# A 90-degree rotation on one core: pairs of slabs turned in place, and 24 transfers in place of 40

## The chip, the core and the metric

The kernel runs on one core of a Trainium2 chip. The core has a matrix engine (TensorE, not used here), VectorE (DVE in the profile), ScalarE (ACT), GpSimd (POOL) and SyncE (SP), and 16 transfer engines (DMA) that move data between the chip's main memory (HBM) and the core's own memory (SBUF, 128 partitions). A second small memory, PSUM, has 128 partitions of 16 KB; transfers here go between HBM and SBUF only, so what is in PSUM must be copied to SBUF before it is stored.

The metric is device time in microseconds, lower is better. Before the change it is 123.27 us, the median of 3 runs (123.24 to 123.33).

## The reference

```python
def setup_inputs():
    batch, c, h, w = 32, 3, 256, 256
    return {"x": np.random.randn(batch, c, h, w).astype(np.float32)}

def reference(x: np.ndarray) -> np.ndarray:
    return np.rot90(x, k=-1, axes=(-2, -1)).astype(np.float32)
```

Each of the 96 images of 256 x 256 single-precision numbers is turned by 90 degrees clockwise. Nothing is computed; 25.17 MB are read, rearranged and written back.

## The kernel before

**Slabs.** Eight images (2048 rows of 1 KB, 2.1 MB) are a slab; there are 12 (`n_slabs`). In SBUF a slab is 128 partitions of 16 KB. Which rows of an image stand in one partition is a choice. With short rows (`short`, 8 image rows) one contiguous piece in HBM is 8 KB and a partition takes two pieces, from two groups of four images (`i`). With long rows (`long`, 16 image rows) a piece is 16 KB and a partition takes one. A long transfer covers every second partition (`units[n][i::I]`), so a slab needs two of them, one for the even and one for the odd partitions.

**Turning.** VectorE's transpose instruction turns blocks of 32 partitions by 32 elements. Its access patterns pick, for each output column, the elements that belong together, and write them back in reversed order. If a slab is loaded in short rows, its turned form stands in long rows, and the other way round: a single slab has 8 KB pieces on one side, the load or the store. Only two slabs turned together as a pair can have 16 KB pieces on both. `turn(n)` (lines 102 to 118) does this with instructions of 128 x 2048 elements, 24 in all.

**Homes.** A turned slab is written where the slab before it was (`home = [turned0] + units[:last]`, line 100): slab 0 goes to PSUM, slab 1 to where slab 0 was, and so on. Slabs 0, 1 and 2 are loaded short and stored long, 3 to 7 loaded long and stored short. Slabs 8 and 9, and 10 and 11, are pairs (`both`, `paired`), loaded and stored long; a pair is turned in four instructions into the place of the pair before it. At the end ScalarE copies slab 0 out of PSUM (line 146) into the place of the last slab, in two halves, and it is stored last.

**Order.** All transfers are issued by SP, one after another, into one queue, which the 16 transfer engines serve in that order. The loads come first, 23 of them (the first half of the last slab is cut into 14 KB and 2 KB rows at line 94). A scheduling note at lines 139 and 140 keeps the first store behind the last loads. Then come the 17 stores: slabs 4, 3, 5, 6, 7 (short, line 132), 1 and 2 (long, line 130), the pairs (lines 124 and 127) and slab 0. A tile framework adds the waits: VectorE waits for the loads of the slab that it turns and, where a new slab overwrites what it has just read, for its own earlier instruction; a store waits for the transposes; and each transfer takes one of eight semaphores in turn, so it waits for the transfer eight before it.

Of the kernel before, what the change touches and what calls it, by code (L numbers as in the profile page):

```python
# [1 line left out]

# [4 lines left out]

@with_exitstack
def kernel(
    ctx: ExitStack,
    tc: tile.TileContext,
    x: bass.AP,
    out: bass.AP,
):

    nc = tc.nc
    fp32 = mybir.dt.float32

    B, C, H, W = x.shape
    P = nc.NUM_PARTITIONS
    RL, RS = 16, 8  # L50
    I = 2
    Q = P * RS // H
    n_slabs = B * C // (Q * I)
    last = n_slabs - 1
    F = RS * W
    long_st = (0, 1, 2)
    both = (8, 10)
    paired = [n + a for n in both for a in range(2)]

    rows_in = x.rearrange("b c h w -> (b c h) w")  # L60
    rows_out = out.rearrange("b c h w -> (b c h) w")

    def short(rows):
        return rows.rearrange("(n i p r) w -> n p i (r w)", i=I, p=P, r=RS)

    def long(rows):
        return rows.rearrange("(n i m r) w -> n i m (r w)", i=I, m=P // I, r=RL)

    ld_short, ld_long, st_short, st_long = short(rows_in), long(rows_in), short(rows_out), long(rows_out)

    units = [None] * n_slabs
    adjacent = [(3, 7), (8, 9), (10, 11)]
    pairs = []
    for us in adjacent + [(u,) for u in range(n_slabs) if all(u not in us for us in adjacent)]:
        pool = ctx.enter_context(tc.tile_pool(name=f"unit{us[0]}", bufs=1))
        held = pool.tile([P, len(us), I * F], fp32, name=f"u{us[0]}")
        for j, u in enumerate(us):
            units[u] = held[:, j]
        pairs.append(held)
    psum = ctx.enter_context(tc.tile_pool(name="psum", bufs=1, space=bass.MemoryType.PSUM))  # L80
    turned0 = psum.tile([P, I * F], fp32, name="turned0")

    def fours(t):
        return t.rearrange("p (i f) -> p i f", i=I)

    for n in (0, 1, 2, 3, 7, 4, 5, 6, *range(8, n_slabs)):
        if n in (1, 2):
            nc.sync.dma_start(out=fours(units[n]), in_=ld_short[n])
            continue
        for i in range(I):  # L90
            if n in long_st:
                ld = nc.sync.dma_start(out=fours(units[n])[:, i], in_=ld_short[n][:, i])  # L92
            else:
                cuts = (0, 14 * W, RL * W) if (n, i) == (last, 0) else (0, RL * W)
                for f0, f1 in zip(cuts, cuts[1:]):
                    ld = nc.sync.dma_start(out=units[n][i::I, f0:f1], in_=ld_long[n, i][:, f0:f1])
                    if f1 == 14 * W:
                        mark = ld

    home = [turned0] + units[:last]  # L100

    def turn(n):
        if n in long_st:
            src = fours(units[n]).rearrange("p i (r g c) -> p c r g i", r=RS, c=RL)
            dst = home[n].rearrange("p (c k r) -> p c r k", c=RL, r=RS)[:, :, ::-1, ::-1]
            parts, step = 2, RL // 2
        elif n in paired:
            if n not in both:
                return
            src = pairs[both.index(n) + 1].rearrange("p a (r g c) -> p c r g a", r=RL, c=RL)  # L110
            dst = pairs[both.index(n)].rearrange("p i (c k r) -> p c r k i", c=RL, r=RL)[:, :, ::-1, ::-1, :]
            parts, step = 4, RL // 4
        else:
            src = units[n].rearrange("p (r g c) -> p c r g", r=RL, c=RS)
            dst = fours(home[n]).rearrange("p i (c k r) -> p c r k i", c=RS, r=RL)[:, :, ::-1, ::-1, :]
            parts, step = 2, RS // 2
        for h in range(parts):
            nc.vector.transpose(out=dst[:, h * step : (h + 1) * step], in_=src[:, h * step : (h + 1) * step])  # L118

    def store(n):  # L120
        if n in paired:
            first = n if n in both else n - 1
            if n == first:
                nc.sync.dma_start(out=st_long[n].transpose([1, 0, 2]), in_=pairs[both.index(n)][::I])
                return
            for i in range(I):
                nc.sync.dma_start(out=st_long[n, i], in_=pairs[both.index(first)][n - first :: I, i])
        elif n in long_st:
            for i in range(I):
                nc.sync.dma_start(out=st_long[n, i], in_=home[n][i::I])  # L130
        else:
            return nc.sync.dma_start(out=st_short[n], in_=fours(home[n]))

    for n in range(both[0]):
        turn(n)
    for n in (4, 3, 5, 6, 7, 1, 2):
        st = store(n)
        if n == 4:
            tc.add_manual_dep(st.ins, mark.ins.name, mybir.DependencyInfo(
                mybir.DependencyClass.Sync, mybir.DependencyReason.SCHED_ONLY), reason="stores after loads")  # L140
    for n in range(both[0], n_slabs):
        turn(n)
        store(n)

    for i in range(I):
        nc.scalar.copy(out=fours(units[last])[:, i], in_=fours(turned0)[:, i])  # L146
    home[0] = units[last]
    store(0)


# [1 line left out]
_INS = ['x']  # L152
_OUTS = [((32, 3, 256, 256), 'float32')]


# [23 lines left out]
```

## Time and profile before

| what | value |
|---|---|
| device time, median of 3 runs | 123.27 us (123.24 to 123.33) |
| span of the profiled execution, first to last instruction | 121.4 us |
| around the span (123.27 less 121.43, if the profiled execution is a median one; the page gives no device time of its own) | 1.84 us |
| VectorE busy | 90.5 us, 24 instructions, from 8.25 to 99.1 us |
| ScalarE busy | 4.9 us, 3 instructions |
| transfer engines' share of the span | 98.0% |
| moved | 25.17 MB read, 25.17 MB written, 414 GB/s over the span |

The profile is one execution, recorded by the chip. Its page gives the busy time of each engine, then the span in 40 slices with the busy share of each engine in tenths, the share of the 16 transfer engines, and the GB/s that they moved. Then it follows the chain of work that ended last back from the end, from each instruction to what released it. "issue" in it is time in which an engine waited for nothing that the profile shows. Lines of groups of instructions read: line of the kernel, engine, operation, output<-input with their sizes, count | busy us, mean ns of one | idle time before them. A window's line reads: from:to, length, busy time and count for VectorE, ScalarE and GpSimd, clock, share of the transfer engines, GB/s. The trace behind the page also has the moments at which each transfer's 16 parts have landed, and the start, duration and size of each packet that a transfer engine moved.

### The profile page before, as it was taken

The page shows a single profiled execution, that of the slowest core. Times are in us where ns is not written, and L with a number is a line of the kernel's source. Part 1 is how long each engine was busy: PE and PEld are TensorE (multiplying, and loading weights), DVE is VectorE, ACT ScalarE, POOL GpSimd, SP SyncE. Part 2 cuts the span into 40 slices and gives each one's busy share as a digit, 9 for nine tenths or more (in the row PEclk, how much of TensorE's full clock was granted, in tenths as well). Part 3 has the DMA queues.
Part 4 walks back from the last instruction along what each step waited for, and adds up shares of the span by engine and source line. Part 5 has one row for each costly group of instructions (what it writes and reads, how often), then busy time and mean ns, then how long its engine had stood idle before and what let it go on. Part 6 is the DMA issues. An engine that isn't in the chain of part 4 may idle for free.

```text
span 121.4 us, 134 instructions
## 1 busy us (share of the span) xinstructions
DVE 90.5 (75%) x24; ACT 4.9 (4%) x3; POOL 0.2 (0%) x4
## 2 busy tenths in 40 slices
DVE  0029999999999999999999999999999960000000
ACT  0000000000000000000040000000000038000000
POOL 0000000000000000000000000000000000000000
DMA  3999999999999999999999999999999999999994
GB/s 84 416 432 424 426 459 432 432 432 426 426 432 426 416 421 432 421 426 450 403 424 426 426 429 429 421 432 424 464 426 432 432 432 432 432 432 432 432 432 178
DMA packets 4800, 50.33 MB, mean 414 GB/s; under 512 B 640, under 2 KB 640, under 8 KB 704
## 3 DMA queue, kind: packets, MB, share of 16 engines
q1 hardware_dynamic: 4800, 50.33, 98.0%
HBM read 25.17 MB, written 25.17 MB: 414 GB/s over the span
## 4 chain that ended last, share of the span: by engine, by line
DVE 55%; issue 17%; DMA 6%; DVEq 3%; ACT 2%; ACTq 1%; SPq 0%
DVE u L118 50%; DVE turned L118 6%; DMA u<-in_x_dram 6%; DVEq L174 3%; ACT u L146 2%; ACTq L174 1%; SPq L92 0%; DVEq L118 0%
## 5 line engine op out<-in xcount | busy, mean ns | idle before, releaser
L118 DVE STREAM_TRANSPOSE u<-u 128x2048 f32<-128x2048 f32 x22 | 83.4, 3861 | 0.3
L118 DVE STREAM_TRANSPOSE turned<-u 128x2048 f32<-128x2048 f32 x2 | 7.1, 3584 | 8.3 <-DMA u<-in_x_dram 8.3
L146 ACT COPY u<-turned 128x2048 f32<-128x2048 f32 x2 | 3.6, 1869 | 35.6 <-DVE u L118 35.6
L146 ACT ACT_TABLE_LOAD x1 | 1.3, 1283 | 62.3 <-DMA u<-in_x_dram 62.3
L163 POOL MEMSET const-uint8-127<- 128x1 uint8 x1 | 0.1, 103 | 0.0
L163 POOL MEMSET const-bfloat16-1.0<- 128x1 bf16 x1 | 0.1, 101 | 0.0
L163 POOL MEMSET const-float32-0.0<- 128x1 f32 x1 | 0.1, 99 | 0.2 <-issue 0.2
L163 POOL MEMSET const-float32-1.0<- 128x1 f32 x1 | 0.1, 99 | 0.0
## 6 DMA issues: line engine op xcount, KB each, us to landing
u<-in_x_dram SPq DMA_DIRECT2D x19, 1024.0 KB, 19.6
out_dram<-u SPq DMA_DIRECT2D x7, 2048.0 KB, 16.3
out_dram<-u SPq DMA_DIRECT2D x10, 1024.0 KB, 18.3
u<-in_x_dram SPq DMA_DIRECT2D x2, 2048.0 KB, 13.7
u<-in_x_dram SPq DMA_DIRECT2D x1, 896.0 KB, 19.3
u<-in_x_dram SPq DMA_DIRECT2D x1, 128.0 KB, 17.2
```

The lines of the kernel that those rows point to most:

```text
L118: nc.vector.transpose(out=dst[:, h * step : (h + 1) * step], in_=src[:, h * step : (h + 1) * step])
L146: nc.scalar.copy(out=fours(units[last])[:, i], in_=fours(turned0)[:, i])
L163: nc = _bacc.Bacc("TRN2", target_bir_lowering=False, num_devices=1)
L174: with _tile.TileContext(nc) as tc:
```

## The change

All 12 slabs are now six pairs, each one tile of 128 x 2 x 4096 elements. PSUM holds two tiles of 8 KB a partition, `spare[0]` and `spare[1]`.

- Slabs 1 and 0 are loaded in short rows, one transfer each, and turned one at a time: slab 1 into the two spares, slab 0 into the place of slab 1; ScalarE then copies the spares to where slab 0 was. Their stores are in 16 KB rows.
- The other ten slabs are loaded as five pairs in 16 KB rows, two transfers a pair, each for every second partition with two pieces (one of each slab, 2 MB apart in HBM). Each pair is turned in its own place, in quarters: the first quarter goes to a spare, the next three each move into the quarter just emptied, and ScalarE copies the spare into the last one in two instructions. The pairs use the two spares in turn.
- All stores are 2.1 MB each in 16 KB rows, in the order of the pairs, after all loads.

SP issues 12 loads and 12 stores, where it issued 23 and 17. VectorE still has 24 transposes, now in other shapes and with a wait for its own previous instruction within a pair. ScalarE has 12 copies in place of 2. The cut of the last slab, the scheduling note and the moving homes are gone.

```diff
-    RL, RS = 16, 8
+    R = 16
...
     def long(rows):
-        return rows.rearrange("(n i m r) w -> n i m (r w)", i=I, m=P // I, r=RL)
+        return rows.rearrange("(n a i m r) w -> n i m a (r w)", a=2, i=I, m=P // I, r=R)
...
-    adjacent = [(3, 7), (8, 9), (10, 11)]
...
-    turned0 = psum.tile([P, I * F], fp32, name="turned0")
+    pairs = [
+        ctx.enter_context(tc.tile_pool(name=f"pair{n}", bufs=1)).tile([P, 2, E], fp32, name=f"u{n}")
+        for n in range(n_slabs // 2)
+    ]
+    spare = [psum.tile([P, E // 2], fp32, name=f"spare{h}") for h in range(2)]
...
-    for n in (0, 1, 2, 3, 7, 4, 5, 6, *range(8, n_slabs)):
...
-                cuts = (0, 14 * W, RL * W) if (n, i) == (last, 0) else (0, RL * W)
...
+    for s, home in ((1, 0), (0, 1)):
+        nc.sync.dma_start(
+            out=pairs[0][:, home].rearrange("p (i f) -> p i f", i=I), in_=ld_short[s])
+    for n in range(1, len(pairs)):
         for i in range(I):
+            nc.sync.dma_start(out=pairs[n][i::I], in_=ld_long[n, i])
...
+    def turn_slab(src, dsts):
+        s = src.rearrange("p (i r g c) -> p c r g i", i=I, r=R // I, c=R)
+        for h, d in enumerate(dsts):
+            d = d.rearrange("p (c k r) -> p c r k", c=hw, r=R // I)[:, :, ::-1, ::-1]
+            nc.vector.transpose(out=d, in_=s[:, h * hw : (h + 1) * hw])
+
+    turn_slab(pairs[0][:, 0], spare)
+    turn_slab(pairs[0][:, 1], [pairs[0][:, 0, : E // 2], pairs[0][:, 0, E // 2 :]])
+    for h in range(2):
+        nc.scalar.copy(out=pairs[0][:, 1, h * E // 2 : (h + 1) * E // 2], in_=spare[h])
+
+    def turn_pair(n):
+        u = pairs[n]
+        src = u.rearrange("p a (r g c) -> p c r g a", r=R, c=R)
+        dst = u.rearrange("p i (c k r) -> p c r k i", c=R, r=R)[:, :, ::-1, ::-1, :]
+        held = spare[n % 2]
+        low, high = slice(0, hw), slice(hw, R)
+        nc.vector.transpose(
+            out=held.rearrange("p (i c k r) -> p c r k i", i=I, c=hw, r=hw)[:, :, ::-1, ::-1, :],
+            in_=src[:, low, low])
+        for c, r in ((low, high), (high, high), (high, low)):
+            nc.vector.transpose(out=dst[:, c, r], in_=src[:, c, r])
+        for i in range(I):
+            nc.scalar.copy(
+                out=u[:, i, : E // 2].rearrange("p (c r) -> p c r", r=R)[:, :, hw:],
+                in_=held[:, i * E // 4 : (i + 1) * E // 4].rearrange("p (c r) -> p c r", r=hw))
+
+    for n in range(1, len(pairs)):
+        turn_pair(n)
+    for n in range(len(pairs)):
+        for a in range(2):
+            if n == 0:
+                st = rows_out[: 2 * P * R].rearrange("(s i m r) w -> i m s (r w)", s=2, i=I, r=R)[a]
             else:
+                st = rows_out.rearrange("(n a i m r) w -> n a m i (r w)", a=2, i=I, m=P // I, r=R)[n, a]
+            nc.sync.dma_start(out=st, in_=pairs[n][a::2])
```

More of the change, by code (lines that the diff above doesn't have):

```diff
@@ L49 @@
     P = nc.NUM_PARTITIONS
-    RL, RS = 16, 8
+    R = 16
     I = 2
[L52 to L58, printed above, removed]
+    E = R * W
+    n_slabs = B * C * H // (P * R)
+    hw = R // 2
     rows_in = x.rearrange("b c h w -> (b c h) w")
@@ L63, in short @@
     def short(rows):
-        return rows.rearrange("(n i p r) w -> n p i (r w)", i=I, p=P, r=RS)
+        return rows.rearrange("(n i p r) w -> n p i (r w)", i=I, p=P, r=R // I)
     def long(rows):
-        return rows.rearrange("(n i m r) w -> n i m (r w)", i=I, m=P // I, r=RL)
-    ld_short, ld_long, st_short, st_long = short(rows_in), long(rows_in), short(rows_out), long(rows_out)
-    units = [None] * n_slabs
-    adjacent = [(3, 7), (8, 9), (10, 11)]
[L73 to L79, printed above, removed]
@@ L80 @@
-    psum = ctx.enter_context(tc.tile_pool(name="psum", bufs=1, space=bass.MemoryType.PSUM))
-    turned0 = psum.tile([P, I * F], fp32, name="turned0")
-    def fours(t):
-        return t.rearrange("p (i f) -> p i f", i=I)
-    for n in (0, 1, 2, 3, 7, 4, 5, 6, *range(8, n_slabs)):
-        if n in (1, 2):
-            nc.sync.dma_start(out=fours(units[n]), in_=ld_short[n])
-            continue
-        for i in range(I):
-            if n in long_st:
-                ld = nc.sync.dma_start(out=fours(units[n])[:, i], in_=ld_short[n][:, i])
-            else:
-                cuts = (0, 14 * W, RL * W) if (n, i) == (last, 0) else (0, RL * W)
[L95 to L147, printed above, removed]
@@ L148 @@
-    store(0)
+        return rows.rearrange("(n a i m r) w -> n i m a (r w)", a=2, i=I, m=P // I, r=R)
+    ld_short, ld_long, st_long = short(rows_in), long(rows_in), long(rows_out)
+    pairs = [
+        ctx.enter_context(tc.tile_pool(name=f"pair{n}", bufs=1)).tile([P, 2, E], fp32, name=f"u{n}")
+        for n in range(n_slabs // 2)
+    ]
+    psum = ctx.enter_context(tc.tile_pool(name="psum", bufs=1, space=bass.MemoryType.PSUM))
+    spare = [psum.tile([P, E // 2], fp32, name=f"spare{h}") for h in range(2)]
```

## The prediction

> **What bounds the kernel now.** I read the engine totals first, then the busy share by slices, then the chain that ended last, then windows cut at the landings of the transfers. First the totals and the slices (a slice is 3.03 us):
>
> ```profile
> DVE 90.5 (75%) x24; ACT 4.9 (4%) x3; POOL 0.2 (0%) x4
> ...
> DVE  0029999999999999999999999999999960000000
> ...
> DMA  3999999999999999999999999999999999999994
> GB/s 84 416 432 424 426 459 432 432 432 426 426 432 426 416 421 432 421 426 450 403 424 426 426 429 429 421 432 424 464 426 432 432 432 432 432 432 432 432 432 178
> DMA packets 4800, 50.33 MB, mean 414 GB/s; under 512 B 640, under 2 KB 640, under 8 KB 704
> q1 hardware_dynamic: 4800, 50.33, 98.0%
> ```
>
> The transfer engines are full from the first slice to the last; VectorE (DVE), the only busy compute engine, stops at 99.1 us, 22 us before the end. Every byte must cross: 25.17 MB in, 25.17 MB out. So the chain that ended last must not be read as "VectorE is the limit":
>
> ```profile
> DVE 55%; issue 17%; DMA 6%; DVEq 3%; ACT 2%; ACTq 1%; SPq 0%
> ```
>
> It follows who released whom. The last stores were issued at 102.8 and 104.0 us but landed at 118.2 and 120.6 us, so they queued for data engines. Only two things can move the end: the rate at which the queue moves, or a gap in it. The rate, in windows cut at landings (two 8 KB-row loads; the 16 KB-row loads; the five 8 KB-row stores; the 16 KB-row stores):
>
> ```profile
> 8.20:18.10 9.90, 9.81 (x3) 0.00 (x0) 0.00 (x0) 1.00 1.03 438
> 18.10:62.10 44.00, 43.83 (x12) 0.00 (x0) 0.00 (x0) 1.00 1.00 425
> 62.20:86.60 24.40, 24.30 (x8) 1.28 (x1) 0.00 (x0) 1.00 1.02 430
> 86.60:120.60 34.00, 12.47 (x4) 3.63 (x2) 0.00 (x0) 1.00 0.98 420
> ```
>
> The columns are window, length, VectorE, ScalarE, GpSimd, clock, transfer share, GB/s. The last window loses its final half microsecond to landing, and packets are booked whole, so to 1% I trust the landing times instead: the first slab (2.1 MB) at 8.15 us, slab 1 at 13.12, slab 2 at 18.09, the last load at 62.17, the last 8 KB-row store at 86.57, the last store at 120.62. These make the sum.
>
> **The change part by part.** The built program has 2 + 10 loads and 12 stores, 24 transfers of 2.1 MB for 40 (the short description says 25).
>
> *Loads.* Before, the two slabs after the first took 4.967 and 4.971 us in 8 KB rows. A 16 KB-row load of 1 MB lands every 2.446 us (seventeen whole steps between 18.09 and 62.17), so 4.892 a slab; one MB cut into 14 KB and 2 KB rows took 2.490. After, one slab after the first is in 8 KB rows and ten in 16 KB rows: 8.15 + 4.97 + 10 x 4.892 = 62.04, against 62.17: -0.13 us. What no row shows is a 16 KB-row load whose 64 partitions each take two pieces 2 MB apart in HBM. The bounds are 4.865 (mean 16 KB-row store: 34.05 us for seven slabs) and 4.97 (the 8 KB-row load, itself two pieces a partition): -0.27 to +0.78 us on ten slabs. I take 4.892, same rows, same direction.
>
> *Stores.* Five slabs leave 8 KB rows. Those took 24.40 us for five, 4.880 each, the switch from reading to writing (0.04 us) included. The two 2 MB stores of before that have the changed kernel's form (64 partitions, two 16 KB pieces each) took 4.872 and 4.871; pairs of 1 MB stores 4.849 to 4.869. After: 0.04 + 12 x 4.872 = 58.50 against 58.45 now: +0.05 us. The row length buys nothing in the stores by these intervals.
>
> *Packet times, the other end.* The trace's packet records have a median of 309 ns for 8 KB, 611 ns for a 16 KB store, 613 ns for a 16 KB load, 540 and 84 ns for the 14 and 2 KB rows, 9 ns for a semaphore packet. Per engine that is 80 x 309 - 40 x 611 = 280 ns for the stores, 16 x 309 - 8 x 613 = 40 for the load slab, 4 x 11 = 44 for the cut, 16 x 9 = 144 for the transfers saved: -0.51 us. But sixteen 8 KB records add to 4.94 us where the store landed in 4.87: records overlap, so I take the landings and keep -0.51 as an end.
>
> *Sixteen transfers fewer.* The landing intervals show no fixed cost: two 1 MB stores 4.86, one of 2 MB 4.87. Zero is taken; the cover is the queue, which is always filled ahead, and if it ran dry each gap would show whole. A rule of the Trainium skill, "DMA: Bandwidth & Descriptors", section "Anatomy of one DMA — SWDGE (gpsimd) path", gives each transfer about 2.0 us of fixed time (fitted to software-generated transfers); sixteen of them would make -32 us, an estimate by that page; the intervals contradict it for queued transfers. The same page, in "Latency and other measured facts", has a rule against this change: 16 KiB rows whose HBM pitch is a large power of two fall to 207 GB/s at 512 KiB and 164 at 2 MiB. By it the ten loads would take some 128 us rather than 49, an estimate again; here the large step is only between the two pieces of a partition, and the store with a 1 MB step landed at 430 GB/s, so I do not follow it.
>
> *First transfer.* It is one of 2 MB instead of two of 1 MB; VectorE's first wait needs the same bytes (first slab) as now. Issues took 407 + 417 ns against 434 for the two-piece form; the first packets began 1.77 us into the span, engine by engine up to 2.66. I take zero, with 0.15 us either way, a sixth of that stagger.
>
> *VectorE.* It keeps 24 transposes. The first four have the forms of today's first four: 8.25 to 23.2 us. New is a wait: the first transpose of the first pair writes `spare1`, which ScalarE must first copy out, and ScalarE's two copies must wait for the fourth transpose, since they write the slab it reads. Copies of 1.87 us, starting 1.76 us apart, end at 26.87: 3.65 us of idle VectorE with everything on it queued behind, and only the stores wait for that. A pair is then one transpose into PSUM (3.58, row below) and three in SBUF, each waiting for the one before: today's form with 64-byte steps on both sides means 3.686, and 3.72 start to start where a wait follows. 3.61 + 3 x 3.72 = 14.8 a pair, 73.9 for five: VectorE ends at 100.8.
>
> ```profile
> L118 DVE STREAM_TRANSPOSE u<-u 128x2048 f32<-128x2048 f32 x4 | 15.6, 3992 | 0.1
> L118 DVE STREAM_TRANSPOSE turned<-u 128x2048 f32<-128x2048 f32 x1 | 3.6, 3561 | 0.0
> ...
> L118 DVE STREAM_TRANSPOSE u<-u 128x2048 f32<-128x2048 f32 x8 | 28.8, 3686 | 0.1
> ```
>
> (The first two are the stretch 15.3 to 31.05 us, the third 70.2 to 99.1.) The bound above is 3.99 to 4.01 (other strides).
>
> *ScalarE.* Ten copies of 1024 elements more. Half of 1.76 us each, 0.1 for the end: a pair's two take 1.9 us. For pairs 1 to 4 they lie under the next pair's first transpose, which writes the other spare; for the last they are exposed to VectorE but not to the queue: 102.7.
>
> *SP's queue.* All loads are issued once the fourth transfer has landed (about 23 us). Each store waits for VectorE, ScalarE and the transfer eight before it. Pair 0 is ready at 26.9, then pairs at about 44, 58, 73, 88 and 102.7 us. The queue reaches them at 62, 72, 82, 91, 101 and 110.8. The last store needs 1.05 us from issue to its first packet (as the first load of today), so 103.8 against 110.4: 6.6 us of cover. The loads of pairs 1 to 5 land at 23, 33, 43, 52 and 62, before VectorE wants each. Nothing here is on the path.
>
> **Sum.** -0.13 + 0.05 + 0 = -0.08 us on the span of 121.43. The page gives no device time of its own execution; against the median, 1.84 us lie around the span, and the runs shown lie within 0.09. So about 123.19; with a little of the packet saving I say 123.17.
>
> **Rivals.** *Packets count in full* (123.27 - 0.51 = 122.76): for it, 8 KB loads do land 1.6% slower than 16 KB ones; against it, the stores' intervals. *Two-piece loads run like today's two-piece loads* and end slower: at 4.97 a slab the loads end at 62.8, 0.65 us later, 123.27 + 0.65 + 0.05 = 123.97. For it, the only loads with two pieces a partition are those slow ones; against it, two pieces cost the stores 0.01 us. It decides from 4.905 us a slab, where the load phase gains nothing, and counts as slower from 4.925. *The in-place chain is late*: the cover of 6.6 us over 20 transposes is 0.33 us each, 3.72 to 4.05. If all 20 take today's slowest 4.01 plus 0.035 for the wait, VectorE ends at 107.9, the copies at 109.8, first packet 110.9: 0.5 us of gap, 123.7; each further 0.1 us per transpose is 2 us. For it, dependent steps and new strides; against it, the 3.69 row.
>
> **How the numbers follow.** Likeliest: the queue keeps its rate, 0.50, by itself 122.95 to 123.40. Packets in full 0.25, two-piece loads 0.13, late chain 0.07, anything else 0.05 (slower). The bound of the classes is 0.2%, 0.25 us, about what a measurement of this kernel can tell from no change: faster is under 123.02. From the likeliest 0.10 falls below it, 0.37 inside, 0.03 above. Faster is 0.10 and nine tenths of the packet case, 0.33; slower is 0.03 and the three slow cases (0.25) less 0.04 for those that stay small, 0.24; the same is what remains, 0.43. The range, 122.7 to 124.0, holds the packet case and the slow loads at their full price.
>
> **What would show it.** Right: loads landing by 62.0, stores 4.87 us apart without a gap, VectorE idle 3.6 us near 23 us, its last transpose near 101. A load step of 4.97 shows the second rival; a hole in the transfer slices after 100 us the third; steps near 4.83 the first. A later first landing than 8.15 would make the start wrong.

## The result and the profile after

The changed kernel takes 122.98 us (median of 21 runs, 122.86 to 123.33), the kernel before 123.21 (21 runs, 123.03 to 123.33). The ratio is 0.9986 with a 95% interval of 0.998 to 0.9993: a gain of about 0.17 us, inside the 0.2% that the prediction counted as the same time. A second set of runs gave 0.9992 (0.9983 to 1.0). So a large rewriting of the transfers moved the time by one part in seven hundred, and the study is about where the parts of that sum lie.

The page of the changed kernel, in the lines that answer to those shown before:

```profile
span 121.2 us, 125 instructions
...
DVE 86.6 (71%) x24; ACT 14.5 (12%) x13; POOL 0.2 (0%) x4
...
DVE  0029999619999999999999999999999970000000
ACT  0000400380000330005000060000600023000000
...
DMA  4999999999999999999999999999999999999994
GB/s 87 403 419 433 465 433 433 427 427 433 433 411 422 416 427 433 433 433 433 422 433 433 433 433 433 433 433 433 433 433 433 433 427 427 433 433 433 433 433 184
DMA packets 3713, 50.33 MB, mean 415 GB/s; under 512 B 385, under 2 KB 385, under 8 KB 385
...
q1 hardware_dynamic: 3712, 50.33, 97.9%
...
DVE 60%; issue 13%; DMA 6%; ACT 2%; ACTq 1%
...
L82 DVE STREAM_TRANSPOSE u<-u 128x2048 f32<-128x2048 f32 x15 | 54.3, 3619 | 0.5
L78 DVE STREAM_TRANSPOSE spare<-u 128x2048 f32<-128x2048 f32 x5 | 17.9, 3574 | 3.7 <-ACT u L70 3.7
L84 ACT COPY u<-spare 128x1024 f32<-128x1024 f32 x10 | 9.6, 1014 | 64.6 <-DVE u L82 64.6
```

Three readings. The packets fell from 4800 to 3713 and the mean rate rose only from 414 to 415 GB/s: the transfer engines were full and are full, and fewer packets are nearly the same bytes per second. VectorE's new pause is there (the dip to 6 and 1 in its slices, 3.7 us before line 78, released by ScalarE's line 70); the kernels with late transposes below show that such a pause costs nothing. The chain that ended last gives VectorE 60% of the span, more than before, though VectorE works 4 us less: it still follows releases, not limits.

The trace has the moment when the last of a transfer's 16 parts lands. Cut at these, a span has four stretches. All numbers below are from one profiled execution of each kernel, in us; "loads" runs from the first slab's landing to the last load's (eleven slabs), "tail" from the last landing to the end of the span:

| kernel | first slab | loads | stores | tail | span |
|---|---|---|---|---|---|
| before | 8.15 | 54.02 | 58.45 | 0.81 | 121.43 |
| changed | 8.24 | 53.91 | 58.24 | 0.81 | 121.20 |
| difference | +0.09 | -0.11 | -0.21 | 0.00 | -0.23 |

### The profile page after: what moved, and what is told of

Read it like the earlier page. It is cut to its first block, busy times and chain, and to the rows that moved or that the text cites. A ratio compares the mean times of both kernels' runs of the same rounds, so it can differ in the third digit from the quotient of the medians.

```text
span 121.2 us, 125 instructions
## 1 busy us (share of the span) xinstructions
DVE 86.6 (71%) x24; ACT 14.5 (12%) x13; POOL 0.2 (0%) x4
## 2 busy tenths in 40 slices
DMA packets 3713, 50.33 MB, mean 415 GB/s; under 512 B 385, under 2 KB 385, under 8 KB 385
## 4 chain that ended last, share of the span: by engine, by line
DVE 60%; issue 13%; DMA 6%; ACT 2%; ACTq 1%
DVE u L82 33%; DVE spare L78 15%; DVE u L65 6%; DMA u<-in_x_dram 6%; DVE spare L65 6%; ACT u L70 2%; ACT u L84 1%; ACTq L123 1%
## 5 line engine op out<-in xcount | busy, mean ns | idle before, releaser
L82 DVE STREAM_TRANSPOSE u<-u 128x2048 f32<-128x2048 f32 x15 | 54.3, 3619 | 0.5
L78 DVE STREAM_TRANSPOSE spare<-u 128x2048 f32<-128x2048 f32 x5 | 17.9, 3574 | 3.7 <-ACT u L70 3.7
L84 ACT COPY u<-spare 128x1024 f32<-128x1024 f32 x10 | 9.6, 1014 | 64.6 <-DVE u L82 64.6
L65 DVE STREAM_TRANSPOSE spare<-u 128x2048 f32<-128x2048 f32 x2 | 7.1, 3585 | 8.3 <-DMA u<-in_x_dram 8.3
L65 DVE STREAM_TRANSPOSE u<-u 128x2048 f32<-128x2048 f32 x2 | 7.8, 3986 | 0.0
L70 ACT COPY u<-spare 128x2048 f32<-128x2048 f32 x2 | 3.6, 1869 | 8.7 <-DVE u L65 8.7
```

The source lines that it names most:

```text
L65: nc.vector.transpose(out=d, in_=s[:, h * hw : (h + 1) * hw])
L70: nc.scalar.copy(out=pairs[0][:, 1, h * E // 2 : (h + 1) * E // 2], in_=spare[h])
L78: nc.vector.transpose(out=held.rearrange("p (i c k r) -> p c r k i", i=I, c=hw, r=hw)[:, :, ::-1, ::-1, :], in_=src[:, low, low])
L82: nc.vector.transpose(out=dst[:, c, r], in_=src[:, c, r])
L84: nc.scalar.copy(out=u[:, i, : E // 2].rearrange("p (c r) -> p c r", r=R)[:, :, hw:], in_=held[:, i * E // 4 : (i + 1) * E // 4].rearrange ...
```

## The experiments

There were 12 runs. What is compared by time is compared with the control in the same set or, across sets, by the ratio to the kernel before.

**The control.** The changed kernel once more, for a second time and a second trace.

> The changed kernel once more, as the control of this set and for a second trace. Theory Q (the queue of transfers moves at a rate that the landing intervals show): 122.98 us give or take 0.1; loads land 4.89 to 4.90 us apart, and if the faster stores of the first four pairs (4.83 to 4.85 us against 4.86 to 4.87 of the last two) belong to the kernel and not to one execution, they are there again. Rival P (packet times count in full): the same time; it cannot tell these.

It took 123.10 us (123.25 for the kernel before). The stretches are 8.34, 53.91, 58.23 and 0.82: loads and stores repeat to 0.01 us, the start does not (+0.10). The first four pairs' faster stores are there again (after the first, 4.82 to 4.87 us a transfer, then mostly 4.86).

**The number of transfers alone.** Loads of pairs and all stores are cut in two, rows as they are.

```diff
-            nc.sync.dma_start(out=pairs[n][i::I], in_=ld_long[n, i])
+            for a in range(2):
+                nc.sync.dma_start(out=pairs[n][i::I, a], in_=ld_long[n, i][:, a])
...
-            nc.sync.dma_start(out=st, in_=pairs[n][a::2])
+            for b in range(2):
+                nc.sync.dma_start(out=st[:, b], in_=pairs[n][a::2, b])
```

> Each load of a pair and each store is cut into two of 1 MB, one 16 KB piece a partition each: 46 transfers for 24, the same rows. Theory Q: no fixed cost of a transfer in a full queue, within 0.1 us of the changed kernel. Rival P: 22 more semaphore packets of 9 ns on every engine, +0.2 us. The rival of two-piece loads: one piece a partition would be faster by up to 0.03 us a slab, -0.3 us on ten slabs.

It took 123.44, 0.34 more than the control, more than any of the three said. The stretches (8.40, 53.99, 58.39, 0.94) put at most 0.08 into the loads and 0.16 into the stores; some 0.12 is in the tail, which none of the three had. One piece a partition did not make the loads faster, so the two-piece load costs nothing that can be seen.

**The row length alone, in the stores and in the loads.**

```diff
-            nc.sync.dma_start(out=st, in_=pairs[n][a::2])
+            for f in range(2):
+                e = slice(f * E // 2, (f + 1) * E // 2)
+                nc.sync.dma_start(out=st[:, :, e], in_=pairs[n][a::2, :, e])
```

(the same for the loads in the other kernel)

> Each store is cut into two of 1 MB by halves of its rows: 8 KB pieces instead of 16 KB in all twelve slabs of stores, loads untouched. Theory Q, from the 4.873 us that 8 KB-row stores took in the kernel before against the 4.853 that the changed kernel's stores took: +0.2 us on 12 slabs. Rival P: 16 x 309 - 8 x 611 = 56 ns a slab, +0.67 us, and +0.1 for the transfers.

> Each load of a pair is cut into two of 1 MB by halves of its rows: 8 KB pieces in the ten slabs loaded in pairs, stores untouched. Theory Q, from the 4.96 us of an 8 KB-row load against 4.895: +0.65 us on ten slabs. Rival P: 16 x 309 - 8 x 615 = 24 ns a slab, +0.24 us, and +0.1 for the transfers.

Stores in 8 KB rows: 123.92, +0.82; the stores stretch 58.76, +0.53, and the tail 1.07, +0.25. Loads in 8 KB rows: 123.98, +0.88; the loads stretch 54.69, +0.78, the tail 0.92, +0.10. For the loads theory Q was near in the stretch (0.65 expected) and the packet times as expected were not: a slab in 8 KB rows takes 0.08 us more, transfers included. For the stores both missed: 0.53 lies between 0.2 and 0.77. Of it, twelve more transfers explain at most 0.16 (the kernel with the transfers alone cut), so the row length costs at least 0.37, some 31 ns a slab. It does buy something in the stores.

**The row length, further.** Quarters in place of halves, loads and stores.

> Each load of a pair and each store is cut into four by quarters of its rows: 4 KB pieces, 90 transfers. If what 8 KB rows cost is a price of each packet, 34 ns a slab of stores for 8 packets more on an engine and 70 ns a slab of loads, then 24 packets more cost 12 x 0.10 + 10 x 0.21 = 3.3 us, and 66 transfers 0.6: 126.9 us. If the price is not by packets but comes with the cutting itself (two transfers where one was), +1 to +1.5 us: 124.0 to 124.5.

It took 127.54, 0.6 above the packet price and far from the other end. Its page:

```profile
DMA  4999999999999999999999999999999999999993
GB/s 81 412 425 429 409 411 407 411 409 409 409 409 411 411 408 411 411 408 411 411 416 421 418 418 421 420 420 420 422 418 417 420 421 420 421 421 418 420 420 147
DMA packets 13217, 50.35 MB, mean 401 GB/s; under 512 B 1440, under 2 KB 1440, under 8 KB 12704
...
DMA 61%; DVE 12%; SPq 3%; issue 3%; ACT 1%; ACTq 1%
```

The engines are as full as ever and move 409 GB/s in loads, 420 in stores, where the changed kernel's slices read 433 for most of both (by its landings, 428 in loads and 432 in stores). The loads stretch is 56.16 (+2.25). With 24 packets more a slab on each engine that is 9.4 ns a packet; the 8 KB loads gave 0.78 over ten slabs and 8 packets, 9.7 ns. In these two kernels transfers grow in step with packets; that the price is the packets' follows from the kernel with the transfers alone cut, where ten more loads cost at most 0.08. The stores stretch is 60.31 (+2.07), but one engine fell back 0.4 us in a single step there and landed last from then on, so 7 ns a packet is an upper end; by the 15th of each transfer's 16 parts the stretch is 1.65 longer than the control's, 5.7 ns a packet, and 8 KB stores gave 5.5.

The packet records of these kernels say nearly the same for the loads. With their medians, 312 ns for 8 KB, 161 for 4 KB and 615 for 16 KB, ten slabs come to 0.72 and 2.32 us more, against 0.78 and 2.25 measured: what went wrong in the expectation for the loads was the 309 ns that it took for an 8 KB packet, more than the way of counting. For the stores (309, 159 and 611 ns) the records come to 0.67 and 2.40, above the 0.53 and 2.07 measured.

**The tail.** In the four kernels above that cut transfers the tail grew, by 0.10 to 0.25 us. The trace shows why. SP ends the program with a row of five waits, which between them ask for the transfers' eight semaphores, in an order that does not depend on which transfer is last; each takes about 0.06 us even when its transfers have long landed. Which semaphore the last transfer uses follows from the number of transfers modulo eight. Two kernels test it: four or eight loads cut in two, so 28 or 32 transfers.

```diff
-            nc.sync.dma_start(out=pairs[n][i::I], in_=ld_long[n, i])
+            for a in range(2) if n >= 4 else (slice(None),):
+                nc.sync.dma_start(out=pairs[n][i::I, a], in_=ld_long[n, i][:, a])
```

(`n >= 2` in the second)

> The four loads of pairs 4 and 5 are cut into two of 1 MB: 28 transfers, so the last one uses the semaphore that SP waits for first at the end. Theory T (SP's last waits stand in a fixed order, 0.06 us each, and those behind the wait that ends last are paid after the last landing): four waits more after the last landing, +0.25 us, and 4 x 9 ns for the transfers: 123.35 to 123.4. Rival (each transfer costs some 15 ns, since 22 more cost 0.34 us): +0.06 us, 123.1 to 123.2.

> The eight loads of pairs 2 to 5 are cut into two of 1 MB: 32 transfers, so the last one uses the semaphore that SP waits for last, as in the changed kernel. Theory T: +0.07 us, 8 x 9 ns, no tail: 123.1 to 123.2, faster than the kernel with 28 transfers by 0.2. Rival (15 ns a transfer): +0.12, slower than the kernel with 28 by 0.06.

The kernel with 28 took 123.26 (ratio 1.0005, 0.9996 to 1.0015), the one with 32 took 123.01 (0.9985, 0.9976 to 0.9993): four transfers more, and 0.25 us less. Tails 1.07 and 0.82. SP's waits, first of the kernel with 28, then with 32 transfers (line, released by: us in total, times, longest):

```profile
SPq L124 <- DMA out_dram<-u: 17.3, 1, 17.3
```

```profile
SPq L124 <- DMA out_dram<-u: 17.2, 4, 4.8
```

With 28, SP's first wait at the end is the one for the last transfer, 17.3 us long, and every other wait of the row comes after it. With 32 the row is worked off while the last transfers run. Theory T is shown. It is also why the kernels above look dearer than their loads and stores (46, 34 and 90 transfers leave two waits behind, 36 leave four). Both the kernel before (40) and the changed one (24) have multiples of eight, so it plays no part in their difference. The 32 transfers cost nothing against 24: the loads stretch is 53.91 in both.

**VectorE's cover.** The first transpose of the last pair is done three or five times instead of once.

```diff
-        nc.vector.transpose(
+        for _ in range(3 if n == len(pairs) - 1 else 1):
+          nc.vector.transpose(
```

> The first transpose of the last pair is done three times, two of them for nothing: +7.3 us of VectorE. Theory Q: the copies end at 108.5, the first packet of the last stores would come 1.9 us after its issue (as the kernel with four more needed), at 110.5, where the queue reaches them at 110.3: 0 to 0.3 us, 123.0 to 123.4. Rival (VectorE is the path): +7.3 us, 130.4.

> The first transpose of the last pair is done five times, four of them for nothing: +14.4 us of VectorE ahead of the last two stores; transfers untouched. Theory Q (VectorE has cover, and only a gap in the queue moves the end): VectorE ends at 113.6, the copies at 115.6, the first packet of the last stores 1.05 us later at 116.7, where the queue would reach them at 110.3: a gap of some 6.3 us, 129.3 us. Rival (VectorE is the path, as the chain of work that ended last reads): all 14.4 us show, 137.4.

With two more, 7.3 us of VectorE, the kernel took 123.17, a ratio of 0.9992 (0.9983 to 1.0001) to the kernel before, as the control. With four more it took 129.86, not 137.4. The page of the first:

```profile
DVE 93.9 (77%) x26; ACT 14.5 (12%) x13; POOL 0.2 (0%) x4
...
DMA  4999999999999999999999999999999999999994
...
DVE 66%; issue 13%; DMA 6%; ACT 2%; ACTq 1%
```

The second, its rates and the window of the hole (no transfer at all, VectorE and ScalarE at work):

```profile
DMA  4999999999999999999999999999999999205995
GB/s 95 409 434 442 434 429 434 419 434 429 434 419 429 429 434 424 424 434 429 429 424 439 434 419 439 429 439 409 450 429 429 434 434 429 102 0 245 409 409 245
```

```profile
110.60:116.90 6.30, 3.27 (x1) 1.93 (x2) 0.00 (x0) 1.00 0.00 0
```

The last copy, which the last two stores wait for, ended at 108.6 and 115.8 us. In the first kernel the queue never noticed. In the second the queue's last packet ended at 110.51 and the next began at 117.11, 1.25 us after the store's issue (not the 1.9 us that the expectation for two more transposes names): a hole of 6.6 us (6.3 expected), and the time is 6.8 longer than the control's by the ratios (1.0542, 1.0528 to 1.0557). So the cover, the time by which the last stores are ready before the queue reaches them, is 7 to 8 us, and the transfer engines are the limit; the chain says "DVE 66%" for a kernel in which 7.3 us of VectorE are free.

**The start.** Over ten traces of kernels whose first load is one transfer on SP, the first slab lands between 8.10 and 8.43 us (mean 8.29); before, with two transfers, at 8.15. So the first load was cut as before.

```diff
+        dst = pairs[0][:, home].rearrange("p (i f) -> p i f", i=I)
+        if s == 1:
+            for i in range(I):
+                nc.sync.dma_start(out=dst[:, i], in_=ld_short[s][:, i])
+            continue
```

> The first load (slab 1) is cut into two of 1 MB as in the kernel before; all else as changed, 25 transfers. Theory S (the later start, 8.24 to 8.40 us to the first slab in five traces against 8.15 before, comes from the two-piece form of the first load): the first slab lands at 8.15 to 8.2, some 0.1 us earlier, and 0.07 come back at the end, since the 25th transfer uses a semaphore that is waited for one wait earlier; 123.05 us. Rival: the start differs from execution to execution; lands at 8.2 to 8.4, and the time is 123.1 to 123.2.

> The kernel with the first load in two once more. Its last load landed 5.26 us after the one before, where the changed kernel took 4.90, and one engine stayed 0.7 us behind from there. If that belongs to the kernel, it is there again, and the time is 123.3 to 123.4. If it was one execution, the step is 4.9 and the time 123.0 to 123.2 (0.07 of tail, 0.1 of earlier start).

The first slab landed at 8.06 and 8.04, even a little before what theory S said; but the kernel took 123.36 and, the second time, 123.22 (ratios 1.0015 and 0.9994), no better than the changed kernel and likely worse. Both traces show where it went: the last load landed 5.26 and 5.11 us after the one before (4.90 in the changed kernel), with 12 and 18 packets of over 640 ns, up to 1148, at 60 us, in the last load before the queue turns to stores; the changed kernel has 6, up to 899, the kernel before none. Nor was the loss one engine's, as the second expectation has it: in the first trace eight of the 16 parts landed 0.46 to 0.70 us behind the earliest from there on, in the second the 16 landings, taken in their order, all came later, by 0.04 to 0.22. The late last load came in both traces of this kernel; but slow packets alone do not make it: the changed kernel's second trace has one, and the kernel with 32 transfers has 11, up to 804, and lost nothing in its loads. Why these packets are slow, and why they cost this kernel more, I did not settle.

**Two issuers at the start.** The second load is issued by ScalarE, at the same time as SP's first.

```diff
-        nc.sync.dma_start(
+        (nc.sync if s else nc.scalar).dma_start(
             out=pairs[0][:, home].rearrange("p (i f) -> p i f", i=I), in_=ld_short[s])
```

> The second load (slab 0) is issued by ScalarE while SP issues the first, all else as changed. If the late engines at the start (up to six of sixteen begin 0.6 us after the others) wait for descriptors of one issuer, both slabs land up to 0.3 us earlier together and the end with them: 122.7 to 122.9. If they wait for something else, no change: 122.95 to 123.15. VectorE starts some 3 to 5 us later in either case, inside its cover.

It took 122.99 (ratio 0.9983, 0.9974 to 0.9991), within the changed kernel's own spread. The two first slabs landed together, at 12.9 and 13.8 us, and the third at 18.07 where the changed kernel has 18.09: no gain. No kernel of this study is measurably better than the changed one.

## Why the prediction was right, and where its steps were not

The forecast was 123.17 us and "the same"; 122.98 and a ratio of 0.9986 are that. The main reading, a queue that is full from end to end so that only its rate or a hole can move the end, is shown by the two kernels with late transposes. By the steps:

- *Loads*: predicted -0.13 with 4.892 us a slab; measured -0.11 (4.895). Right. The two-piece loads cost nothing: the second rival is out.
- *Stores*: predicted +0.05, measured -0.21 (between -0.09 and -0.23 over nine traces with these stores as they are, all against the one trace before). This is the step that failed: "The row length buys nothing in the stores by these intervals". It rested on two landing intervals of 4.87 us for the form with two 16 KB pieces; twelve of that form, in two traces, average 4.853, and single steps scatter from 4.82 to 4.91. The kernel with 8 KB stores prices the row length at some 31 ns a slab, 0.15 us for five slabs. The landings agree in size: the first five stores took 24.40 us before, in 8 KB rows, and 24.25 to 24.33 in those nine traces. The remaining 0.06 fits five fewer transfers, at up to 13 ns each, but is within the scatter of the stretch (58.23 to 58.36 for stores that no edit touched).
- *Packets in full*, the first rival: predicted -0.51. The loads and stores together gained 0.32. Its direction was right in the stores, its size was not (0.28 us for their rows, against some 0.15), and for loads it under-priced rows (40 ns a slab by the prediction, 24 by the later expectation, some 80 measured), since it took 309 ns for an 8 KB packet where the loads of pairs show 312.
- *Sixteen transfers fewer*: predicted zero. Eight more in the loads cost nothing; 22 more cost at most 0.24 us outside the tail. Near zero. The fixed 2.0 us a transfer of the Trainium skill ("DMA: Bandwidth & Descriptors", section "Anatomy of one DMA — SWDGE (gpsimd) path"), a fit to software-generated transfers, would be 44 us for those 22, by estimate; in a queue that never runs dry the traces show none of it. Its rule on large powers of two ("Latency and other measured facts") is for the pitch from partition to partition. These loads have 16 KB there and 2 MB only between the two pieces of a partition, so they do not test it; they land 2.1 MB in 4.895 us, 428 GB/s.
- *First transfer*: predicted zero within 0.15. Measured +0.09 in the profiled execution, and about 0.2 in the mean over ten traces against three with two transfers (8.04 to 8.15). This term was under-sized, and it ate part of what the stores gained. That the two errors have opposite signs is why the sum is nearer than its parts; that is luck, and no part of the reasoning.
- *VectorE*: the pause was 3.7 us (predicted 3.65), the transposes in SBUF 3.62 us (predicted 3.69), the end 99.2 (predicted 100.8). *ScalarE*: a pair's two copies 1.92 us (predicted 1.9). The cover was put at 6.6 us; it is over 7. The third rival is out.

## What to carry to other kernels

Where the transfer engines are full, read a change by landing times, stage by stage, over whole stages: one or two intervals of one form scatter by as much as the effect looked for. A packet more costs each engine about 10 ns in loads and 5 to 7 in stores here: rows of 4 KB in place of 16 KB, in both directions, cost 3.6% of the time, rows of 8 KB some 0.6% in the loads and 0.4% in the stores. No run here has pieces longer than 16 KB. The chain that ended last names who released whom; only added work, or a hole in the transfer slices, shows whether that engine is the limit.

## What the runs showed that was not expected

- The number of transfers modulo eight decides how many waits of 0.06 us follow the last landing: 0.82 us of tail at 24 and 32 transfers, 1.07 at 28 and 36. The difference is more than the whole gain of the change.
- At the turn from loads to stores some load packets take up to 1148 ns in place of 614. Where all pieces are of 16 KB there, a trace has between none and 18 of over 640 ns, and the changed kernel's own two traces have 6 and 1. Their cause is open.
- Between zero and six of the 16 engines begin about 0.6 us after the others, differently from execution to execution. That does not explain when the first slab lands: with none late it came at 8.40 and 8.43 us (the two kernels with late transposes), with four late at 8.10 (32 transfers). Issuing from a second engine did not change the end.
